# Expert stage of a hybrid encoder block: transposes placed inside the preceding product, splits on VectorE alone, two row blocks of each down matrix in full fp32

## The chip, the cores and the metric

The kernel runs on one core of a Trainium2 chip. Times are device microseconds (us) of one execution. Three runs of the kernel before gave 1526.49, 1527.76 and 1528.14 us; their median is 1527.76 us. In the text PE is TensorE (PEld its weight loads), DVE is VectorE, ACT is ScalarE, POOL is GpSimd, and SP is the engine whose queue issues most DMAs.

## The reference

One encoder layer on 1024 tokens of width 1024, all in float32. Three mixers (cross-attention to a memory, a convolution module, a bidirectional RWKV-7 recurrence) share one input projection and one output projection. Then comes the part that the change touches, a mixture of sixteen experts in which each expert picks its 128 tokens, and at last a norm:

```
h   = rms_norm(x)
aff = softmax(h @ w_router)                    # 1024 tokens x 16 experts
gates, idx = top_k(aff per expert, 128)
xe  = h[idx]                                   # 16 x 128 x 1024
hid = silu(xe @ w_gate) * (xe @ w_up)          # each w: 16 x 1024 x 1024
ye  = (hid @ w_down) * gates
x   = x + scatter_add(ye at idx)
y   = rms_norm(x)
```

## The kernel before, in words

The mixers, the output projection and the router's products come first; they fill the span up to about 860 us. Nothing there is touched. Then each expert's tokens are chosen (L1361 to L1407), which is a chain of short VectorE instructions, and the sixteen experts follow one by one.

**Products.** Every expert has three products of 128 rows with a 1024x1024 matrix: gate, up and down. A product takes eight steps k, one for each block of 128 rows of the matrix, and in each step two halves n of 512 columns. Both factors are split into a high part h and a rest l of the type float32r, and `mm3` (L331 to L333) adds three products: high x high, high x rest, rest x high. So one product has 8 x 2 x 3 = 48 matmuls and one expert 144. A matmul of two plain float32 factors is not split.

**Weights.** `fetch_w` (L1250) loads 256 rows of a matrix (1 MB) into one of twelve rooms `eraw`, in a fixed rotation, from SP's queue; the rooms hold one expert's twelve loads. The generator `parts` (from L1341) makes the two parts of each block of 128 rows: ScalarE copies the high part `ewh` (L1351, L1355), and the rest `ewl` is a subtraction. For gate and up it is always VectorE's (L1356, with the norm's gain). For down the subtractions alternate between VectorE and POOL (L1352). There are five buffers each of `ewh` and `ewl`, so the splits run up to five steps ahead of PE. The first five are made by L1360, ahead of the choice of tokens in the program.

**Rows.** `fetch(e)` makes a one-hot matrix `oneh` on VectorE (L1414), multiplies it with the token numbers and gates (L1418, eight small matmuls), copies the index and the gates on VectorE (L1419, L1420), and gathers the rows `xe` with an indirect DMA from POOL (L1422). `transposed` turns 128 rows into the stationary factor of a product: eight PE transposes into two PSUM banks (L1434), and for each bank ScalarE's high part (L1436, `xh` or `fh`) and VectorE's rest (L1437, `xl` or `fl`).

**Order.** For expert e the program has: the up product; the gating `hid` (L1545, two halves on VectorE, which read the up product's PSUM); the transposes of the next expert's rows; the fetch of the rows of expert e + 2; the gate product of expert e + 1 with its silu on ScalarE (L1458); the transposes of the gated product; the down product; ScalarE's scaling by the gates `ye` (L1471) and an indirect DMA from POOL that adds the rows to `x2_d` in DRAM (L1472). A planner orders the instructions of each engine ahead of time by the order of the program and by its own costs; on the chip each engine runs its own in that order.

**The end.** The gate product of the last expert is interrupted after four steps by the down product of the last but one. `last_loads` loads all rows of `x2_d` once that expert's rows have been added (L1493), and the last matrix. While the last products run, the rows are squared (L1506, L1508), scaled on VectorE (L1513) and stored (L1517). After the last down product, `last_norm` does the same for the last expert's 128 rows (L1523 to L1529).

Of the kernel before, what the change touches and what calls it, by code (L numbers as in the profile page):

```python
# [12 lines left out]
F32 = mybir.dt.float32  # L13
# [74 lines left out]
GD = 2  # L88
NPRE = 2
NBOR = 0  # L90
# [8 lines left out]
PF1 = 9  # L99


@with_exitstack
def hybrid_block_kernel(ctx: ExitStack, tc: tile.TileContext, x, xT, memT, memn, w_in, w_mk, w_mv, pcols,
# [14 lines left out]
    # ---------------------------------------------------------------- constants  # L118
# [16 lines left out]
    # mask of the within-chunk matrices, [rows s (twice), {strict, inclusive}, t]  # L135
    mask = const.tile([P, 2, C], F32, name="mask")
    V.memset(mask, 1.0)
    for hf in range(2):
        r = slice(hf * 64, hf * 64 + 64)
        for q in range(2):  # L140
            # keeps t - s - 1 + q >= 0
            G.affine_select(out=mask[r, q, :], in_=mask[r, q, :], pattern=[[1, C]], compare_op=ALU.is_ge, fill=0.0,
                            base=q - 1, channel_multiplier=-1)
# [8 lines left out]
    # masks that put the inverses of the diagonal blocks in place: [row, parity, block column]  # L152
# [19 lines left out]
    # identity columns as the lanes of the inversion hold them: [lane (quadrant, parity, chunk), sigma, t]  # L172
# [5 lines left out]
    # derived per-channel columns  # L178
# [27 lines left out]
    def rsqrt(dst, src, scale, eps):  # L206
        """dst = (src * scale + eps) ** -0.5: a first guess from the exponent, then Newton's steps."""
# [18 lines left out]
    def run(mains, fills):  # L226
        """mains: names in order; fills: name -> (pieces, number, first, last, needs); pieces of fills are spread over
        the mains' steps. needs: (own piece, name, count)"""
# [24 lines left out]
    # tiles that live through the whole first part  # L253
# [4 lines left out]
    # ---------------------------------------------------------------- projections  # L258
# [16 lines left out]
    # the even taps, the odd ones, and their sums  # L275
# [59 lines left out]
    # memory: keys and values  # L335
# [3 lines left out]
    def memory():  # L339
# [15 lines left out]
        # a bank's first product alone starts it: where nothing was written yet, the others' first ones do not add  # L355
# [76 lines left out]
    def ev_shift(nm, j):  # L432
        st = {}

        def f(ps, n, sl):
# [6 lines left out]
            if n == 1:  # L442
# [3 lines left out]
                if nm in shifted:  # L446
                    # rows 64-127 belong to the backward scan: reversed time
# [8 lines left out]
                if nm == "gd":  # L456
                    # twice the sigmoid
# [15 lines left out]
    # the first two projections follow the loads  # L473
# [30 lines left out]
    # ---------------------------------------------------------------- convolution  # L504
# [3 lines left out]
    def taps(eng, i, j):  # L508
        """one of the three half-rate filters of a tile of channels: even taps on even tokens, odd on odd, and
        their sums on neighbours' sums"""  # L510
# [17 lines left out]
    def conv():  # L528
        for i in range(3):
# [8 lines left out]
            # even tokens, then odd ones  # L538
# [50 lines left out]
    def keep(i, n):  # L589
        """a part of the mixers' output, split in two, to DRAM"""  # L590
# [8 lines left out]
    # ---------------------------------------------------------------- attention  # L599
# [47 lines left out]
    # ---------------------------------------------------------------- RWKV-7  # L647
    # The backward scan is the forward one on reversed time: its tiles hold time reversed, so one step serves both.
# [7 lines left out]
    def early():  # L656
        """what the first chunks need, in the room of the convolution and the attention"""
# [9 lines left out]
        # zeros stand where one head's rows meet the other head's columns  # L667
# [10 lines left out]
        # restart marks of the running sums  # L678
# [6 lines left out]
    def late():  # L685
        """the rest, in the room of the projections"""
# [6 lines left out]
        # of these two, the last half pair needs the second only  # L693
# [9 lines left out]
    def swap():  # L703
        """room for the output projection, for the last half pair"""
# [29 lines left out]
    def chunks(ap, d):  # L734
        """[P, 512] as [P, chunk, t], in the time of direction d"""
        ap = ap if d == 0 else ap[:, ::-1]
        return ap.rearrange("p (a b) -> p a b", b=C)
# [3 lines left out]
    def spread(rs):  # L741
        """[P tokens, 4 tiles, head] to [channels, 512 tokens] in PSUM"""
# [8 lines left out]
    def columns(src, two, ps=None):  # L751
        """512 tokens' products with two columns, tokens on partitions"""
# [24 lines left out]
    def prep(p, k, g):  # L777
# [7 lines left out]
        for d in range(2):  # L785
# [23 lines left out]
            # 1/P overwrites the running sums  # L809
# [4 lines left out]
            # -kk a / P  # L814
# [8 lines left out]
            # the even head's rows hold k before b, the odd one's b before k  # L823
# [16 lines left out]
    def bonus(p):  # L840
        # each token's r . k of both directions, weighed by r_k
# [5 lines left out]
    def within(g):  # L847
        """within-chunk matrices"""
# [13 lines left out]
    def prep2(p, k, g):  # L862
        BT = g["BT"] = Z["BT"][g["u"] % 2]
        SV = g["SV"] = Z["SV"][g["u"] % 2]
        for d in range(2):
            n = k if d == 0 else 1 - k
            # b and k with tokens on partitions
# [7 lines left out]
            # values with tokens on partitions: rows 0-63 the even head, rows 64-127 the odd one  # L875
# [13 lines left out]
    def invert(g):  # L889
        # inverses of the 32 x 32 diagonal blocks of I - A, one block and column parity per lane  # L890
# [9 lines left out]
        # lanes (quadrant, parity, chunk): [t, s]  # L900
        Lt = Z["ew"].tile([P, 32, 32], F32, name="Lt", bufs=1)
        V.transpose(Lt.rearrange("p a b -> p (a b)"), Ld[:, :, None, :].to_broadcast([P, 32, 2, NCH]))
        Dt = Z["ew"].tile([P, 16, 32], F32, name="Dt", bufs=1)      # [sigma, t]
# [12 lines left out]
        # back to rows s, columns t, both parities placed by the masks  # L916
# [9 lines left out]
        # the first block, not transposed  # L926
# [84 lines left out]
    def gated(p, n, pl, g):  # L1011
        """the gate with the norm's weight, and with what stands beside the norm"""
# [12 lines left out]
    def normed(p, ns, gl, out):  # L1025
        """both halves' (or one's) group norm, what stands beside it, the gate, and the split for the last product"""
# [42 lines left out]
    def residual():  # L1069
        """x plus the part of the output projection that the attention and the convolution give"""  # L1070
# [85 lines left out]
    def routed(dst, src):  # L1156
        """the products of 128 rows with the router's weights"""
# [464 lines left out]
```

## Time and profile before

| | |
|---|---|
| median of three runs | 1527.76 us (1526.49 to 1528.14) |
| span of the profiled execution, first to last instruction | 1526.2 us |
| TensorE busy | 1341.4 us |
| VectorE busy | 1230.6 us |
| ScalarE busy | 841.9 us |
| POOL busy | 458.8 us |
| moved by DMA | 327.92 MB |

The profiled execution is one of its own; of its time the page has the span, and the median of the three runs lies 1.6 us above that. Matmuls are pipelined: a matmul's duration holds the run-out of its results, and where they follow each other the distance of their starts is what one costs. A row of the timeline merges equal instructions that follow each other (x8). What stands in brackets is the idle time of the engine just before, and what ended it. A row of the waits has who waited, for whom, us in total, how often, and the longest.

### The profile page before, as it was taken

The numbers are of one execution on the slowest core, as the hardware profiler recorded it, in microseconds if no ns is written. First come the engines' busy times: TensorE is split into PE (matmuls) and PEld (weight loads), VectorE is DVE, ScalarE is ACT, GpSimd is POOL, SyncE is SP. The second block draws the span as 40 slices with busy tenths as digits, with TensorE's granted clock in tenths as the row PEclk, the third lists the DMA queues.
The fourth block names the chain that finished last, engine by engine and source line by source line (L and its number), as shares of the span: only waits on it lengthen the run. The fifth ranks groups of instructions, "written<-read, shape, count | busy, mean of one in ns | idle before, by whom it ended". The sixth has DMA issues, their size and how long they took to land.

```text
span 1526.2 us, 24448 instructions
## 1 busy us (share of the span) xinstructions
PE 1341.4 (88%) x9254; PEld 1074.2 (70%) x9254; DVE 1230.6 (81%) x2071; ACT 841.9 (55%) x1209; POOL 458.8 (30%) x302
## 2 busy tenths in 40 slices
PE   6988999996889898788999279999999999999984
PEld 4776658675777777667778167777777777777763
DVE  8899975698686979697534879888888888888887
ACT  4222574434435353424312358888888888888872
POOL 2233313432121213121211004444444444444323
PEclk9998899997897988899899679999999999999996
DMA  8222113313443524333525769999999999999855
GB/s 287 73 63 65 57 63 130 126 56 117 115 139 96 155 93 137 105 111 116 206 115 227 297 223 329 367 361 361 365 367 361 368 370 355 364 365 368 323 174 225
DMA packets 146101, 327.92 MB, mean 215 GB/s; under 512 B 9792, under 2 KB 64960, under 8 KB 145984
## 3 DMA queue, kind: packets, MB, share of 16 engines
q1 hardware_dynamic: 139360, 303.14, 55.3%
q0 software_dynamic: 6192, 22.55, 5.2%
q8 instruction: 72, 1.18, 0.3%
q10 hardware_dynamic: 432, 0.68, 0.1%
q14 instruction: 45, 0.37, 0.1%
HBM read 288.58 MB, written 37.75 MB: 214 GB/s over the span
## 4 chain that ended last, share of the span: by engine, by line
PE 55%; DVE 23%; ACT 8%; DMA 6%; issue 5%; POOL 1%; SPq 0%; POOLq 0%; DVEq 0%; ACTq 0%
PE mm L331 14%; PE mm L333 14%; PE mm L332 13%; DVE cv L519 3%; DVE dtmp L912 3%; DVE Dt L913 2%; DMA fo<-oT_d 2%; ACT Ld L897 2%; DVE ewl L1356 1%; ACT hid L1458 1%; ACT ewh L1351 1%; PE mm L1167 1%; PE mm L747 1%; DMA eraw<-in_w_ed_dram 1%; PE psA L856 1%
## 5 line engine op out<-in xcount | busy, mean ns | idle before, releaser
L1356 DVE SCALAR_TENSOR_TENSOR ewl<-eraw,pc,ewh 128x1024 fp32r<-128x1024 f32 x256 | 336.3, 1362 | 20.4 <-ACT ewh L1355 18.8
L1355 ACT ACTIVATE ewh<-eraw,pc 128x1024 fp32r<-128x1024 f32 x256 | 290.4, 1152 | 72.2 <-PE mm L333 70.1
L1352 POOL TENSOR_TENSOR ewl<-eraw,ewh 128x1024 fp32r<-128x1024 f32 x64 | 183.6, 2874 | 131.9 <-ACT ewh L1351 115.8
L331 PE MATMUL mm<-ewh,xh 128*128 128x512 f32 x512 | 201.6, 394 | 12.6 <-ACT xh L1436 12.6
L332 PE MATMUL mm<-ewl,xh 128*128 128x512 f32 x512 | 199.8, 390 | 0.0
L333 PE MATMUL mm<-ewh,xl 128*128 128x512 f32 x512 | 198.1, 392 | 0.1
L1351 ACT ACTIVATE ewh<-eraw 128x1024 fp32r<-128x1024 f32 x128 | 136.0, 1064 | 44.9 <-PE mm L333 39.0
L1352 DVE TENSOR_TENSOR ewl<-eraw,ewh 128x1024 fp32r<-128x1024 f32 x64 | 122.5, 1915 | 35.6 <-ACT ewh L1351 34.2
L331 PE MATMUL mm<-hh,wh 128*128 128x512 f32 x304 | 127.2, 419 | 9.8 <-ACT hh L312 9.8
L333 PE MATMUL mm<-hh,wl 128*128 128x512 f32 x304 | 126.5, 416 | 0.8 <-POOL wl L327 0.8
L332 PE MATMUL mm<-hl,wh 128*128 128x512 f32 x304 | 126.5, 416 | 0.4 <-DVE hl L313 0.3
L331 PEld LDWEIGHTS mm<-ewh,xh 128*128 128x128 f32 x512 | 96.3, 188 | 36.2 <-ACT xh L1436 16.5
L331 PE MATMUL mm<-ewh,fh 128*128 128x512 f32 x256 | 102.7, 403 | 14.3 <-ACT fh L1436 8.5
L332 PEld LDWEIGHTS mm<-ewl,xh 128*128 128x128 f32 x512 | 96.4, 188 | 19.6
L333 PEld LDWEIGHTS mm<-ewh,xl 128*128 128x128 f32 x512 | 95.0, 188 | 19.5 <-DVE xl L1437 0.6
L332 PE MATMUL mm<-ewl,fh 128*128 128x512 f32 x256 | 102.1, 399 | 7.0 <-DVE ewl L1352 7.0
L333 PE MATMUL mm<-ewh,fl 128*128 128x512 f32 x256 | 99.1, 397 | 1.8 <-DVE fl L1437 1.8
L327 POOL TENSOR_TENSOR wl<-wraw,wh 128x512 fp32r<-128x512 f32 x38 | 59.1, 1559 | 126.7 <-ACT wh L326 109.0
L1422 POOL DMA_INDIRECT xe<-h_d,idx x16 | 29.4, 1836 | 217.0 <-DVE gates L1420 217.0
L967 POOL TENSOR_TENSOR sps<-S,pcs 128x128 f32<-128x128 f32 x48 | 22.8, 474 | 218.7 <-DVE S L993 115.4
L331 PEld LDWEIGHTS mm<-hh,wh 128*128 128x128 f32 x304 | 60.1, 198 | 26.2 <-ACT hh L312 10.4
L332 PEld LDWEIGHTS mm<-hl,wh 128*128 128x128 f32 x304 | 60.0, 197 | 18.5 <-DVE hl L313 3.0
(412 smaller groups left out, 3011.2 us busy)
## 6 DMA issues: line engine op xcount, KB each, us to landing
eraw<-in_w_eg_dram SPq DMA_DIRECT2D x64, 1024.0 KB, 8.6
eraw<-in_w_eu_dram SPq DMA_DIRECT2D x64, 1024.0 KB, 9.2
eraw<-in_w_ed_dram SPq DMA_DIRECT2D x64, 1024.0 KB, 5.7
fo<-oT_d SPq DMA_DIRECT2D x64, 320.0 KB, 3.9
wraw<-in_w_in_dram SPq DMA_DIRECT2D x38, 256.0 KB, 2.7
ld_k<-d_k SPq DMA_DIRECT2D x18, 256.0 KB, 3.3
ld_v<-d_v SPq DMA_DIRECT2D x18, 256.0 KB, 3.1
xk<-in_xT_dram SPq DMA_DIRECT2D x16, 256.0 KB, 4.7
```

The costliest lines, as they stand in the source:

```text
L327: G.tensor_sub(wl, raw, wh.bitcast(F32))
L331: T.matmul(ps, lhsT=lh, rhs=rh, start=first, stop=False)
L332: T.matmul(ps, lhsT=lh, rhs=rl, start=False, stop=False)
L333: T.matmul(ps, lhsT=ll, rhs=rh, start=False, stop=last)
L519: V.scalar_tensor_tensor(o[:, 0:ln], z, w, o[:, 0:ln], op0=ALU.mult, op1=ALU.add)
L897: A.copy(Ld[r_, :, c:c + 4].rearrange("p t c -> p c t"), g["AM", d, q][r_, :, h, 0, b * 32:b * 32 + 32])
L912: IE.tensor_tensor(tmp[:, sg, ts], lcol, drow, op=ALU.mult)
L913: IE.tensor_tensor(Dt[:, sg, ts], Dt[:, sg, ts], tmp[:, sg, ts], op=ALU.add)
L1351: A.activation(h, raw[a], AF.Copy)
L1352: eng.tensor_sub(l, raw[a], h.bitcast(F32))
L1355: A.activation(h, raw[a], AF.Copy, scale=gain)
L1356: V.scalar_tensor_tensor(l, raw[a], gain, h.bitcast(F32), op0=ALU.mult, op1=ALU.subtract)
```

## The change

It has three parts, and moves the first five splits.

1. The transposes of the next expert's rows are issued after step 3 of the up product (`KTX`), and those of the gated product after step 2 of the next expert's gate product (`KTH`), each within the product's matmuls. The fetch of the rows of expert e + 2 is issued after step 0 of that gate product (`KTF`). The last expert's gated product is transposed ahead of its down product, as before.
2. All subtractions of the splits are VectorE's.
3. The last two (`NWHOLE`) of the eight row blocks of each down matrix are not split. PE multiplies them as they were loaded, with an unsplit copy `fw` of the transposed rows that ScalarE makes, as plain float32 matmuls. They use no `ewh` or `ewl` buffer, and their room `eraw` is read by PE.
4. The first five splits are issued within `fetch(0)`, and on VectorE behind its L1420 (the gates of the first expert), rather than ahead of the choice of tokens.

Comments were taken out as well. The core of the diff:

```diff
-GD = 2
+NWHOLE = 2
+KTX, KTF, KTH = 3, 0, 2
...
             for a in range(2):
+                if src is w_ed and k2 * 2 + a >= KT - NWHOLE:
+                    yield raw[a], None
+                    continue
                 h, l = halves.pop(0) if halves else [ex.tile([P, FF], F32R, name=n, bufs=NWB) for n in ("ewh", "ewl")]
-                turn[0] += 1
-                eng = G if turn[0] % GD == 0 else V
                 if src is w_ed:
                     A.activation(h, raw[a], AF.Copy)
-                    eng.tensor_sub(l, raw[a], h.bitcast(F32))
+                    V.tensor_sub(l, raw[a], h.bitcast(F32))
...
-    split = [next(parts) for _ in range(NWB)]
+    split = []
...
         if e == 0:
             tc.keep_in_program_order(g)
+
+            with tc.issue_after(gs.ins):
+                split.extend(next(parts) for _ in range(NWB))
...
-    def transposed(src, nm):
-        h = ex.tile([P, KT, P], F32R, name=nm + "h", bufs=2 if nm == "x" else 1)
-        l = ex.tile([P, KT, P], F32R, name=nm + "l", bufs=2 if nm == "x" else 1)
+    def transposed(src, nm, whole=0):
+        h = ex.tile([P, KT - whole, P], F32R, name=nm + "h", bufs=2 if nm == "x" else 1)
+        l = ex.tile([P, KT - whole, P], F32R, name=nm + "l", bufs=2 if nm == "x" else 1)
+        w = ex.tile([P, whole, P], F32, name=nm + "w", bufs=1) if whole else None
...
-            s_ = slice(a * 4, (a + 1) * 4)
-            A.activation(h[:, s_, :], ps, AF.Copy)
-            V.tensor_tensor(l[:, s_, :], ps, h[:, s_, :].bitcast(F32), op=ALU.subtract)
-        return h, l
+            n = min(4, max(0, KT - whole - a * 4))
+            s_ = slice(a * 4, a * 4 + n)
+            if n:
+                A.activation(h[:, s_, :], ps[:, 0:n], AF.Copy)
+                V.tensor_tensor(l[:, s_, :], ps[:, 0:n], h[:, s_, :].bitcast(F32), op=ALU.subtract)
+            if n < 4:
+                i = a * 4 + n - (KT - whole)
+                A.copy(w[:, i:i + 4 - n], ps[:, n:])
+        return h, l, w
...
-                mm3(acc[n], xh[:, k, :], xl[:, k, :], h[:, sl], l[:, sl], k == 0, k == KT - 1)
+                if l is None:
+                    T.matmul(acc[n], lhsT=xw[:, k - KT + NWHOLE], rhs=h[:, sl], start=k == 0, stop=k == KT - 1)
+                else:
+                    mm3(acc[n], xh[:, k, :], xl[:, k, :], h[:, sl], l[:, sl], k == 0, k == KT - 1)
...
-        product(up, *cur, then)
+        else:
+            then = {KTX: [lambda: turn_x(e + 1)]}
+        product(up, *xs.pop(e), then)
...
-            cur = transposed(rows.pop(0), "x")
+            then = {KTF: [lambda: bring(e + 2)] if e + 2 < NE else [], KTH: [lambda: turn_h(e, done)]}
             if e + 2 < NE:
-                rows.append(fetch(e + 2))
-                hid = gate(e + 1, cur)
-                add_back(e, done)
+                hid = gate(e + 1, xs[e + 1], then)
+                add_back(e, hs.pop(e))
```

`turn_x(e)` is `transposed` of the rows of expert e, `turn_h` that of the gated product with `whole=NWHOLE`, and `bring` is `fetch`.

## Rows read from the trace of the kernel before

**Rows 1.** The page, part 1: busy us (share of the span) and instructions of each engine.

```profile
PE 1341.4 (88%) x9254; PEld 1074.2 (70%) x9254; DVE 1230.6 (81%) x2071; ACT 841.9 (55%) x1209; POOL 458.8 (30%) x302
```

**Rows 2.** Busy time by window, one expert's period (columns in the first line).

```profile
core 0: us, PE busy (x) PEld busy (x) DVE busy (x) ACT busy (x) POOL busy (x), PEclk, DMA share, GB/s
1066.98:1104.60 37.62, 36.19 (x169) 29.55 (x168) 33.27 (x30) 30.76 (x32) 15.59 (x6) 1.00 1.01 364
```

**Rows 3.** Timeline of PE, end of an up product: start us, us, instruction, [idle before].

```profile
1095.08 0.39 PE L331 MATMUL mm<-ewh,xh 128*128 128x512 f32 x1
...
1104.37 0.39 PE L333 MATMUL mm<-ewh,xl 128*128 128x512 f32 x1
1104.60 1.03 PE L1434 MATMUL mm<-ident,xe 128*128 128x128 f32 x8
1106.48 0.50 PE L331 MATMUL mm<-ewh,xh 128*128 128x512 f32 x1 [0.85 <-ACT xh L1436]
1106.82 0.40 PE L332 MATMUL mm<-ewl,xh 128*128 128x512 f32 x1
...
1107.72 1.05 PE L1418 MATMUL mm<-tokaff,oneh 128*128 128x6 f32 x8
1108.63 0.70 PE L333 MATMUL mm<-ewh,xl 128*128 128x512 f32 x2
```

**Rows 4.** Timeline of PE, from a gate product to a down product.

```profile
1118.74 1.03 PE L1434 MATMUL mm<-ident,hid 128*128 128x128 f32 x8
1120.33 0.50 PE L331 MATMUL mm<-ewh,fh 128*128 128x512 f32 x1 [0.55 <-ACT fh L1436]
```

**Rows 5.** Waits from 960 to 1500 us: us in total, times, longest.

```profile
ACT ewh L1355 <- PE mm L333: 62.2, 150, 2.9
...
DVE ewl L1356 <- ACT ewh L1355: 14.5, 28, 0.7
...
PE mm L331 <- ACT xh L1436: 10.9, 13, 0.9
```

**Rows 6.** Timeline of PE, down product of the last but one expert.

```profile
1455.62 0.72 PE L333 MATMUL mm<-ewh,fl 128*128 128x512 f32 x2 [1.75 <-DVE fl L1437]
```

**Rows 7.** Timeline of VectorE, from the end of an up product on.

```profile
1104.47 1.40 DVE L1545 SCALAR_TENSOR_TENSOR hid<-mm,gates,hid 128x512 f32<-128x512 f32 x2
...
1112.90 2.48 DVE L1356 SCALAR_TENSOR_TENSOR ewl<-eraw,pc,ewh 128x1024 fp32r<-128x1024 f32 x2
1115.29 1.22 DVE L1352 TENSOR_TENSOR ewl<-eraw,ewh 128x1024 fp32r<-128x1024 f32 x1
1117.31 2.54 DVE L1352 TENSOR_TENSOR ewl<-eraw,ewh 128x1024 fp32r<-128x1024 f32 x1 [0.80 <-ACT ewh L1351]
```

**Rows 8.** Unsplit fp32 products: the group of L558, and two of its instructions.

```profile
L558 PE MATMUL mm<-oT,o 128*128 128x512 f32 x12 | 5.8, 605 | 0.0
...
228.09 0.59 PE L558 MATMUL mm<-oT,o 128*128 128x512 f32 x1
...
228.52 0.59 PE L558 MATMUL mm<-oT,o 128*128 128x512 f32 x1
```

**Rows 9.** Weights' loads from 1000 to 1440 us; a window with the queues undisturbed.

```profile
DMA to landing us min/median/max: 4.8/7.5/11.0
...
1106.00:1114.00 8.00, 7.48 (x36) 6.01 (x37) 7.12 (x9) 4.89 (x6) 1.84 (x1) 1.00 1.03 417
```

**Rows 10.** Timeline of VectorE, POOL and PE ahead of the first product.

```profile
879.86 6.06 DVE L1356 SCALAR_TENSOR_TENSOR ewl<-eraw,pc,ewh 128x1024 fp32r<-128x1024 f32 x5
...
886.28 1.87 POOL L1422 DMA_INDIRECT xe<-h_d,idx  x1 [31.56 <-DVE gates L1420]
...
891.63 1.94 PE L1434 MATMUL mm<-ident,xe 128*128 128x128 f32 x8 [2.45 <-DMA xe<-h_d,idx]
```

**Rows 11.** The last matrix: the chain's DMA; VectorE's groups from 1491.05 to 1513.75.

```profile
1476.76 15.42 DMA eraw<-in_w_ed_dram
...
L1513 DVE SCALAR_TENSOR_TENSOR eraw<-eraw,fr,gfi 128x1024 f32<-128x1024 f32 x8 | 14.2, 1805 | 0.0
L1352 DVE TENSOR_TENSOR ewl<-eraw,ewh 128x1024 fp32r<-128x1024 f32 x4 | 9.2, 2291 | 0.0
```

More of the change, by code (lines that the diff above doesn't have):

```diff
@@ L1332, in hybrid_block_kernel @@
     ex = pool("ex", bufs=2, side="right")
-    turn = [0]
     halves = [[ex.tile([P, FF], F32R, name=n, bufs=NWB) for n in ("ewh", "ewl")] for _ in range(NWB)]
@@ L1419, in fetch @@
         V.tensor_copy(idx[:, e:e + 1], ps[:, 0:1])
-        V.tensor_reduce(gates[:, :, e], ps[:, 1:5].rearrange("p (a b) -> p a b", b=2), axis=AX.X, op=ALU.add)
+        gs = V.tensor_reduce(gates[:, :, e], ps[:, 1:5].rearrange("p (a b) -> p a b", b=2), axis=AX.X, op=ALU.add)
         xe = ex.tile([P, D], F32, name="xe")
@@ L1434, in transposed, with product @@
                 T.transpose(ps[:, j, :], src[:, (a * 4 + j) * P:(a * 4 + j + 1) * P], ident)
-            s_ = slice(a * 4, (a + 1) * 4)
-            A.activation(h[:, s_, :], ps, AF.Copy)
-            V.tensor_tensor(l[:, s_, :], ps, h[:, s_, :].bitcast(F32), op=ALU.subtract)
-        return h, l
-    def product(acc, xh, xl, then=None, ks=range(KT)):
+            n = min(4, max(0, KT - whole - a * 4))
[7 more added lines that the diff above has]
+        return h, l, w
+    def product(acc, xh, xl, xw, then=None, ks=range(KT)):
         for k in ks:
@@ L1448, in product, with gate @@
                     f()
-    def gate(e, xs, between=None):
+    def gate(e, xs, then=None, between=None):
         ga = [mm("cx") for _ in range(2)]
         if between:
-            product(ga, *xs, ks=range(2 * BRK))
+            product(ga, *xs, then, ks=range(2 * BRK))
             between()
-        product(ga, *xs, ks=range(2 * BRK if between else 0, KT))
+        product(ga, *xs, then, ks=range(2 * BRK if between else 0, KT))
         hid = ex.tile([P, FF], F32, name="hid", bufs=2)
@@ L1459, in gate, with down @@
         return hid
-    def down(e, done, then=None):
-        hs = transposed(done, "f")
+    def down(e, hs, then=None):
         dn = [mm() for _ in range(2)]
@@ L1465, in down, with add_back @@
         return dn
-    def add_back(e, done):
-        dn = down(e, done)
+    def add_back(e, hs):
+        dn = down(e, hs)
         ye = ex.tile([P, D], F32, name="ye", bufs=1)
@@ L1530, in last_norm, with turn_x, turn_h, bring @@
                              in_offset=None)
-    rows = [fetch(0), fetch(1)]
-    cur = transposed(rows.pop(0), "x")
-    hid = gate(0, cur)
+    rows = {0: fetch(0), 1: fetch(1)}
+    xs, hs = {0: transposed(rows[0], "x")}, {}
+    def turn_x(e):
+        xs[e] = transposed(rows.pop(e), "x")
+    def turn_h(e, done):
+        hs[e] = transposed(done, "f", NWHOLE)
+    def bring(e):
+        rows[e] = fetch(e)
+    hid = gate(0, xs[0])
     for e in range(NE):
         up = [mm("y0"), mm("y1")]
-        then = None
         if e == NE - 1:
@@ L1547, in hybrid_block_kernel @@
         if e + 1 < NE:
-            cur = transposed(rows.pop(0), "x")
+            then = {KTF: [lambda: bring(e + 2)] if e + 2 < NE else [], KTH: [lambda: turn_h(e, done)]}
             if e + 2 < NE:
-                rows.append(fetch(e + 2))
-                hid = gate(e + 1, cur)
-                add_back(e, done)
+                hid = gate(e + 1, xs[e + 1], then)
+                add_back(e, hs.pop(e))
             else:
-                hid = gate(e + 1, cur, lambda: (add_back(e, done), last_loads()))
+                hid = gate(e + 1, xs[e + 1], then, lambda: (add_back(e, hs.pop(e)), last_loads()))
         else:
@@ L1557, in hybrid_block_kernel @@
             then[OGK].insert(0, own_gather)
-            dn = down(e, done, then)
+            dn = down(e, transposed(done, "f", NWHOLE), then)
     with tc.manual_schedule():
```

## The prediction

> **What bounds the kernel now.** I read the page first: over the span TensorE is busy 88%, VectorE 81%, ScalarE 55% [rows 1]. The change touches the sixteen experts and the two ends of that stage, so the question is what sets the pace there. The window from one expert's row transposes to the next is 37.62 us long, at a granted clock of 1.00, with PE busy 36.19, VectorE 33.27, ACT 30.76 and a DMA share of 1.01 [rows 2]. Three resources look full; the timeline of PE and the waits tell them apart.
>
> PE issues its split products without a hole: 41 steps from 1095.08 to 1104.37, 0.2266 us each [rows 3]. 144 of them are 32.63 of the 37.62. The other 5.0 lie at the boundaries. The eight transposes of the next rows start at 1104.60 and the first matmul behind them at 1106.48, 1.88 later, of which 0.85 is a wait for ScalarE's copy xh; that matmul takes 0.34 instead of 0.23, another 0.11. The one-hot products of the next list take from 1107.72 to 1108.63, 0.91, and start some 0.2 late. The transposes of the gated product take from 1118.74 to 1120.33, 1.59, with a wait of 0.55 for fh [rows 4], and 0.1 again. These make 4.8, with the products 37.4. So PE, in its own order, sets the pace. Among the waits PE's for xh comes 13 times in the window, once per expert; VectorE's splits wait for ACT, and ACT's for PE to free a buffer, 150 times [rows 5]: both follow PE.
>
> **The change, part by part.** *Transposes inside the product before.* PE still runs 16 per expert, but does not stand behind them. Eight cost at most the group's 1.03 with its run-out, and the eight one-hot products, with matmuls right behind them, 0.91 [rows 3]; I take 0.9. For x that saves 1.88+0.11-0.9 = 1.09 us, for 15 experts 16.4. For the hidden rows 1.59+0.11-0.9 = 0.80, for 14 experts 11.2. The fifteenth has a worse boundary: 1.75 more of waiting for fl [rows 6], which stood on VectorE behind a split; 0.8+1.75 = 2.6 saved. What hides the new waits: the transposes of x come with four of eight steps left, 5.4 us of matmuls, against copies and subtractions of some 2.4; those of the hidden rows come after three steps (3 x 6 x 0.2266 = 4.1) of the next gate product, while VectorE's gating, 1.40, starts as the up product ends [rows 7], so they are ready with 2.7 in hand. If that cover goes, PE waits in the midst of the product, with every later matmul behind it. The list's fetch moves behind the first gate step; its one-hot work and its gather stay, and I count its 0.2 of lateness as staying.
>
> *Two of eight row blocks of each down matrix unsplit.* Per block and half, three steps (0.68) go and one full fp32 product comes. The convolution's norm has such products (L558): two halves by three tiles are 6 in the program and 12 instructions in the trace, so each is two; back to back they step by 0.43, from 228.09 to 228.52 [rows 8]. 0.86-0.68 = 0.18, four times per expert 0.72: for the fifteen experts of the stage 10.8 lost. Bounds: 0.23 per instruction, the split step (0.9 per expert won), and the 0.6 that one lasts alone (2.1 lost). The step of 0.43 is measured back to back, as they will stand, so I take it.
>
> *Splits on VectorE alone.* POOL's four subtractions per expert go; VectorE has six instead of four. One takes 1.22 alone and 2.54 where POOL's overlapped it [rows 7], so the down splits take some 7.3 us per expert where four took about as much: nothing. ScalarE loses two copies and gains a short one. VectorE then has 16 splits of 1.24 (19.8), 7.3, gating 1.4, xl and fl 2.3, the one-hot 1.2 and small change: 32.3 in a period of 36.4. It is tightest over gate and up: 19.8+1.4+2.3+1.5 = 25.0 against PE's 16 x 1.36 + 2 x 0.9 + 0.9 = 24.5. The lead of five buffers, won back in each down product (7.3 against 8.2+3.4), covers the 0.5. So PE is late next, as before.
>
> *Weights.* Twelve rooms hold one expert's twelve loads, and a load is issued when its room comes free, a period ahead of its use. Landing takes 4.8 to 11.0 us [rows 9], so some 22 us are in hand. The last room of each down matrix is now freed by PE's read, not by a split, some 3 us later, and the loads behind it in SP's queue wait with it; that lessens the 22. The queues moved 417 GB/s over 8 us [rows 9] against the period's mean of 364 [rows 2]: its bytes need at least 37.62 x 364/417 = 32.8 us.
>
> The Trainium skill, SBUF — State Buffer, section "A bandwidth-pool intuition that's wrong (but worth ruling out)", puts the path from HBM to a core at about 358 GB/s and calls HBM almost always the bottleneck; by that 364 would be the ceiling and the period could not shrink. The 417 GB/s do not agree with it as a ceiling; what it would do here is the second rival.
>
> *Start.* VectorE does five splits (879.86, 6.06 us) ahead of the first list's index; the first gather starts at 886.28 and the first transposes at 891.63, after 2.45 of waiting for it [rows 10]. Put behind the index, the splits give back up to 4.0 us. But the second list's one-hot then stands behind them, and PE may run its products ahead of the transposes, which leaves 0.4. I take the middle, 2.2.
>
> *End.* The last matrix lands after a chain of DMAs (1476.76 plus 15.42) that PE does not set. From 1491 to 1513.8 VectorE never stops: 8 scalings, 14.2 us, and 4 splits, 9.2, beside POOL's [rows 11]. Without POOL, 8 at 1.24 and 6 at 1.22 are 17.2: 6 less. Against it, eight fp32 instructions after the last landing take 3.4, or 6.9 at the half clock. I take 5; bounds 0 and 6.
>
> **Sum.** 16.4+11.2+2.6-10.8 = 19.4 in the experts, 2.2 at the start, 5 at the end: 26.6. 1526.2-26.6 = 1499.6 of span. The median of the runs stands 1.6 above the profiled span: 1501.
>
> **Rivals.** (1) VectorE becomes the bound over gate and up: if its splits cost 1.32 there (POOL's address work for gather and scatter falls beside them), it is short by 0.5+1.3 = 1.8 per expert, more than the 1.2 won. 15 x 1.2 = 18 of the 26.6 go: 1519. For it: 33.27 of 37.62 busy. Against it: its splits wait for ACT today.
>
> (2) The loads hold their 37.6 us per expert whatever PE does. PE can run ahead by the 22 in hand, which its 21.6 of gain use up; then the end's loads queue behind late weights. Between 1506 (only the end's gain lost) and 1527 (all of it); 1514. For it, the share of 1.01; against it, the 417 GB/s.
>
> (3) Slower: the transposes in the product's midst stand too early in PE's order. They need the gating, and that stands on VectorE behind whatever splits the planner puts ahead of it, 1.24 each; the 2.7 in hand cover two. From the third PE waits; with four ahead 2.3 per expert, 1.1 more than is won, 14 x 1.1 less 7 at the ends: 1536; with six ahead 1570. Against it: the gating starts at once today [rows 7].
>
> (4) The planner, which orders by its own costs, leaves the transposes at the boundaries: the waits stay, fp32 costs 10.8, the ends give 7: 1531.
>
> (5) More than forecast: the one-hot's 0.2 goes in every expert, the start gives 4, the end 6: 1495, and to 1491 where the transposes hide further.
>
> **How the numbers follow.** The forecast, 1495 to 1510, has 0.60; (1) 0.13, (2) 0.08, (3) 0.05, (4) 0.05, (5) 0.09. The range of 1492 to 1518 leaves out (3) and (4) and the far ends of (1), (2) and (5). About 0.2%, 3 us, is what a measurement can tell from no change: of (4) a fifth and of (2) a tenth fall within it. Faster 0.88, same 0.02, slower 0.10.
>
> **What would show it.** After the change: 36.4 us between one expert's x transposes and the next (37.4 or more: wrong); no entry of PE waiting for xh or fh; fp32 instructions in steps of 0.43; down splits on VectorE at 1.22, none on POOL; later landings, but no wait of ACT or PE for a weight; the first gather up to 4 us sooner behind the first one-hot; VectorE through some 6 us sooner after the last matrix lands. The forecast is wrong if PE waits for ewl in the gate and up products, or stands before a transpose in their midst.

## The result, and the profile after

The changed kernel takes 1507.07 us (median; 1499.55 to 1507.65), the one before 1527.12 in the same runs: a ratio of 0.985, 95% interval 0.980 to 0.990. Forecast was 1501. The profiled execution's span is 1505.9 us, 20.3 less than before.

What lies ahead of the experts is the same code in both kernels, but its length varies from run to run (see the last section). So I compare from the first one-hot on VectorE (878.72 us before, 878.38 after) to the last instruction. In all tables here an expert ends where ScalarE's copy of its down product ends.

| stretch, us | before | after | gained | forecast |
|---|---|---|---|---|
| first one-hot to the first gate product | 14.7 | 14.2 | 0.5 | 2.2 |
| to the end of the 11th expert | 427.1 | 410.8 | 16.3 | 12.9 |
| the next four experts | 146.4 | 144.3 | 2.0 | 6.5 |
| from there to the end | 59.3 | 58.2 | 1.1 | 5 |
| sum | 647.5 | 627.6 | 19.9 | 26.6 |

(The forecast's 1.17 per expert, with 1.8 more for the fifteenth, is split as the rows are.) Page row and the window of one steady period, as in [rows 1, 2]:

```profile
PE 1346.2 (89%) x9190; PEld 1064.3 (71%) x9190; DVE 1191.3 (79%) x2103; ACT 806.2 (54%) x1193; POOL 264.2 (18%) x238
```

```profile
1086.00:1122.11 36.11, 36.11 (x165) 28.85 (x164) 31.50 (x31) 29.02 (x31) 3.43 (x2) 1.00 1.00 379
```

The period fell from 37.62 to 36.11, and PE is busy in all of it: the 1.4 us of holes are gone. From 1158 to 1303 us the waits hold no row of PE at all, where [rows 5] had PE waiting for xh once per expert. PE's timeline, at the transposes of x and at the unsplit blocks:

```profile
1090.57 1.03 PE L1443 MATMUL mm<-ident,xe 128*128 128x128 f32 x8
1091.36 0.48 PE L334 MATMUL mm<-ewh,xh 128*128 128x512 f32 x1
1091.67 0.40 PE L335 MATMUL mm<-ewl,xh 128*128 128x512 f32 x1
...
1117.78 3.59 PE L1460 MATMUL mm<-eraw,fw 128*128 128x512 f32 x8
1120.81 0.79 PE L334 MATMUL mm<-ewh,xh 128*128 128x512 f32 x1
1121.45 0.40 PE L335 MATMUL mm<-ewl,xh 128*128 128x512 f32 x1
```

The eight transposes hold the next matmul back by 0.79, where [rows 3] had 1.88, and no bracket stands behind them. The step after it is 0.31 instead of 0.23, so they cost 0.87 in all. From the first unsplit instruction to the second split one behind them are 3.67 us; less one split step of 0.23, eight instructions took 3.44, or 0.43 each.

At the start, VectorE, POOL and PE, as in [rows 10]:

```profile
881.77 6.06 DVE L1360 SCALAR_TENSOR_TENSOR ewl<-eraw,pc,ewh 128x1024 fp32r<-128x1024 f32 x5
887.75 1.22 DVE L1418 TENSOR_TENSOR oneh<-slots,posT 128x1024 fp32r<-128x1024 f32 x1
...
882.07 1.93 POOL L1426 DMA_INDIRECT xe<-h_d,idx  x1 [27.70 <-DVE gates L1424]
...
889.12 1.84 PE L1422 MATMUL mm<-tokaff,oneh 128*128 128x6 f32 x8 [7.53 <-DVE oneh L1418]
890.82 1.97 PE L1443 MATMUL mm<-ident,xe 128*128 128x128 f32 x8
```

The first gather is issued 3.7 us behind the first one-hot instead of 7.6, but PE's queue has the second list's one-hot products ahead of the transposes, and their one-hot stands behind the five splits.

At the end, SP's queue and PE:

```profile
1454.55 2.06 SPq L1509 DMA_DIRECT2D eraw<-x_d  x4
1456.70 0.46 SPq L1253 DMA_DIRECT2D eraw<-in_w_eu_dram  x1
...
1472.34 1.22 PE L334 MATMUL mm<-ewh,xh 128*128 128x512 f32 x2 [9.69 <-ACT ewh L1359]
```

The last block of the last up matrix is now issued behind the four loads of the x2 rows, which wait for the last scatter. Before, it was issued 20.1 us ahead of them (1453.91 against 1474.04). The program text is the same in both kernels (`NLR = 5`) and has this block behind the rows; the planner moved it ahead of them in the kernel before, and does not here. PE stands still 9.7 us in the up product for it.

In the last four experts, PE, ScalarE and VectorE; the first two rows of ScalarE are of a steady period. Below them are ScalarE's waits, the first line from 1122.1 to 1158.2 (steady), the others from 1342.1 to 1380.3:

```profile
1324.75 0.30 PE L1443 MATMUL mm<-ident,xe 128*128 128x128 f32 x1 [1.91 <-DMA xe<-h_d,idx]
...
1154.09 1.15 ACT L1359 ACTIVATE ewh<-eraw,pc 128x1024 fp32r<-128x1024 f32 x1 [0.20 <-PE mm L336]
1156.66 0.69 ACT L1487 ACTIVATE ye<-mm,gates 128x512 f32<-128x512 f32 x1 [1.43 <-PE mm L1460]
...
1371.29 1.14 ACT L1359 ACTIVATE ewh<-eraw,pc 128x1024 fp32r<-128x1024 f32 x1
1378.04 0.69 ACT L1487 ACTIVATE ye<-mm,gates 128x512 f32<-128x512 f32 x1 [5.60 <-PE mm L1460]
...
1379.80 1.28 DVE L1360 SCALAR_TENSOR_TENSOR ewl<-eraw,pc,ewh 128x1024 fp32r<-128x1024 f32 x1 [5.39 <-ACT ewh L1359]
```

```profile
ACT ewh L1359 <- PE mm L336: 4.3, 14, 1.1
...
ACT ye L1487 <- PE mm L1460: 5.6, 1, 5.6
...
ACT fh L1447 <- PE mm L1443: 2.9, 1, 2.9
...
ACT hid L1475 <- PE mm L336: 1.3, 1, 1.3
```

Two things differ from the steady experts. Single transposes of x stand right behind their gather, and PE waits 1.91 us in one. And ScalarE takes the copy of the down product (ye) after one or two splits of the next product instead of five, stands 5.6 us in it, and VectorE then waits as long for its next ewh. The copies fh and hid stand ahead of splits there too. In a steady period ScalarE waits at its splits, for PE to free a buffer; in this one it never does, so its splits no longer fill the buffers ahead of PE.

Four regular experts, less the half gate product that the last one lacks (24 steps), would take 139.0 us; these took 144.3. PE's waits in them sum to 3.9 of the 5.3: 1.9 for the gather, 1.0 for ewh and 1.0 for ewl.

### The profile page after: what moved, and what is told of

Same layout as the page of the kernel before. It is cut to its first block, busy times and chain, and to the rows that moved or that the text cites. A ratio compares the mean times of both kernels' runs of the same rounds, so it can differ in the third digit from the quotient of the medians.

```text
span 1505.9 us, 24196 instructions
## 1 busy us (share of the span) xinstructions
PE 1346.2 (89%) x9190; PEld 1064.3 (71%) x9190; DVE 1191.3 (79%) x2103; ACT 806.2 (54%) x1193; POOL 264.2 (18%) x238
## 4 chain that ended last, share of the span: by engine, by line
PE 59%; DVE 22%; DMA 7%; ACT 5%; issue 4%; POOL 1%; SPq 0%; POOLq 0%; DVEq 0%; ACTq 0%
PE mm L336 13%; PE mm L335 13%; PE mm L334 13%; DVE cv L522 3%; PE mm L1460 3%; DVE dtmp L915 2%; DVE Dt L916 2%; PE mm L1443 2%; ACT Ld L900 2%; DMA fo<-oT_d 2%; DMA eraw<-in_w_ed_dram 1%; PE psA L859 1%; PE mm L1170 1%; DVE BK L831 1%; PE psS L993 1%
## 5 line engine op out<-in xcount | busy, mean ns | idle before, releaser
L1360 DVE SCALAR_TENSOR_TENSOR ewl<-eraw,pc,ewh 128x1024 fp32r<-128x1024 f32 x256 | 319.8, 1280 | 73.0 <-ACT ewh L1359 65.9
L335 PE MATMUL mm<-ewl,xh 128*128 128x512 f32 x512 | 203.0, 396 | 3.0 <-DVE ewl L1360 2.9
L1356 DVE TENSOR_TENSOR ewl<-eraw,ewh 128x1024 fp32r<-128x1024 f32 x96 | 113.1, 1219 | 7.0 <-ACT ewh L1355 5.5
L336 PEld LDWEIGHTS mm<-ewh,xl 128*128 128x128 f32 x512 | 96.8, 189 | 20.1 <-DVE xl L1448 0.2
L1355 ACT ACTIVATE ewh<-eraw 128x1024 fp32r<-128x1024 f32 x96 | 98.6, 1058 | 13.3 <-PE mm L336 9.3
L1488 POOL DMA_INDIRECT x_d<-ye,idx x15 | 25.8, 1721 | 345.7 <-ACT ye L1487 345.7
L336 PE MATMUL mm<-ewh,fl 128*128 128x512 f32 x192 | 74.7, 390 | 1.1 <-DVE fl L1448 1.1
L335 PE MATMUL mm<-ewl,fh 128*128 128x512 f32 x192 | 75.5, 393 | 0.1
L334 PE MATMUL mm<-ewh,fh 128*128 128x512 f32 x192 | 73.3, 390 | 0.0
L522 DVE SCALAR_TENSOR_TENSOR cv<-u,cw,cv 128x512 f32<-128x512 f32 (+1 forms) x87 | 72.2, 860 | 0.1
L336 PEld LDWEIGHTS mm<-hh,wl 128*128 128x128 f32 x304 | 59.6, 196 | 17.1 <-POOL wl L330 3.8
```

Source lines behind the costliest of these rows:

```text
L334: T.matmul(ps, lhsT=lh, rhs=rh, start=first, stop=False)
L335: T.matmul(ps, lhsT=lh, rhs=rl, start=False, stop=False)
L336: T.matmul(ps, lhsT=ll, rhs=rh, start=False, stop=last)
L522: V.scalar_tensor_tensor(o[:, 0:ln], z, w, o[:, 0:ln], op0=ALU.mult, op1=ALU.add)
L1355: A.activation(h, raw[a], AF.Copy)
L1356: V.tensor_sub(l, raw[a], h.bitcast(F32))
```

## The experiments

The theory at the start: the gain is the placement of the transposes, and the shortfall is order, in SP's queue at the end, in PE's in the last four experts, and on VectorE at the start. In the headings, "from the first one-hot" is the time from there to the last instruction (before 647.5, after 627.6). Where no ratio is given, the kernel was run once, and what is said of it is read from that one trace.

### Order of the loads at the end: from the first one-hot 624.1

```
-NLR = 5
+NLR = 6
```

> One number changed: all four blocks of the last up matrix are issued ahead of the four loads of the x2 rows (six blocks instead of five). Theory A (the order of SP's queue took the end's gain): the block that now lands behind the x2 rows no longer waits for the last scatter, the product of the last expert's up matrix loses its stop of 9.7 us, the last transfer of the down matrix lands some 2.5 to 5 us earlier, and the time is 1502 to 1504.5 us against 1507.1 for the changed kernel. Rival B (the same bytes pass the queue behind the scatter either way, so the stop only moves from the up product to the down product): 1506 to 1508.

Ratio to the kernel before 0.986 (0.983 to 0.990). SP and PE at the end:

```profile
1415.62 7.96 SPq L1253 DMA_DIRECT2D eraw<-in_w_eu_dram  x4
...
1454.07 5.05 SPq L1253 DMA_DIRECT2D eraw<-in_w_ed_dram  x4
...
1469.61 1.22 PE L334 MATMUL mm<-ewh,fh 128*128 128x512 f32 x2 [5.41 <-ACT ewh L1355]
1473.57 0.80 PE L335 MATMUL mm<-ewl,fh 128*128 128x512 f32 x1 [2.74 <-DVE ewl L1356]
```

All four blocks are issued long before the scatter, and the stop in the up product is gone. Of its 9.7 us, 5.4 and 2.7 come back in the down product, whose blocks still stand behind the rows. All of PE's waits behind the 15th expert fall from 12.9 to 9.1, and 3.4 us are won from the first one-hot on. Theory A holds for the size, B for most of the stop.

### Splits behind the second one-hot: 625.2

```
-            tc.keep_in_program_order(g)
-            with tc.issue_after(gs.ins):
-                split.extend(next(parts) for _ in range(NWB))
+            tc.keep_in_program_order(g)
+        if e == 1:
+            with tc.issue_after(oh_.ins):    # oh_: this list's one-hot
+                split.extend(next(parts) for _ in range(4))
```

> Four of the first five weight splits are issued behind the second expert's one-hot on VectorE instead of all five ahead of it. Theory A (the start gained only 0.8 us because TensorE takes the second list's one-hot products ahead of the first transposes, and their one-hot stood behind five splits of 1.2 us): the first transposes start at 886.5 to 887.5 us instead of 890.8, the first gate product 4 us earlier than 892.6, the time 1503 to 1504. Rival B (the gather of the first rows or the split of xl, which then stands behind the moved splits, sets the start): under 1.5 us earlier, 1505.5 to 1507.

Ratio 0.985 (0.981 to 0.989). Its first one-hot is at 884.17:

```profile
887.86 1.87 POOL L1426 DMA_INDIRECT xe<-h_d,idx  x1 [27.70 <-DVE gates L1424]
...
893.15 1.94 PE L1443 MATMUL mm<-ident,xe 128*128 128x128 f32 x8 [2.39 <-DMA xe<-h_d,idx]
```

Against that mark the transposes start at 8.98 instead of 12.44, and now they wait for the gather: 3.5 us won at the start, 2.3 of them left at the end. Theory A holds, to the bound that the gather sets. The times expected in absolute terms could not be read, since the stretch ahead varies by more; the median of the whole runs, 1505.6, lies where B had it.

### Transposes of x held, then PE's whole order held: 627.0 and 629.8

```
-                T.transpose(ps[:, j, :], src[...], ident)
+                t = T.transpose(ps[:, j, :], src[...], ident)
+                if nm == "x":                 # second kernel: always
+                    tc.keep_in_program_order(t)
```

> The transposes of x are held in the place where the program text has them, in all experts. Theory A (the last four experts lost 6 us to transposes that were put, one by one, right behind their gather, and to what they displaced): the periods of the last four experts fall from 38.8, 38.2 and 37.4 to 36.1 to 36.6 us, no wait of TensorE for a gather is left, the time is 1500 to 1502. Rival B (these experts are slow since the loads' order changes near the end, whatever the transposes do): the periods stay above 37.3, the time above 1505. Rival C (the experts gain, but the stop at the last up block grows by as much, since its load and the x2 rows come by the same queue): the marks of the last downs are 6 us earlier, the time 1504 to 1507.

> The changed kernel with all transposes and all one-hot products of the experts held in the place where the program text has them, so that TensorE's order is the same in every expert. Theory A (what the last four experts still lost, 4 us with the transposes of x alone held, comes from the order of the work there: one-hot products and h transposes put earlier, and the splits that they displace): the last four periods fall from 144.3 us in all to 139.5 to 141, as four regular ones less the half gate product that is moved behind; from the first one-hot to the end 624 to 626 us against 627.6, since part of it is lost again in the stop at the last up block. Rival B (late transfers, whatever the order): 143 or more.

The second holds the experts' one-hot products as well. First kernel: ratio 0.986 (0.981 to 0.990); PE's waits from 1295 to 1438 us:

```profile
PE mm L335 <- DVE ewl L1360: 1.4, 3, 0.5
PE mm L334 <- ACT ewh L1359: 1.0, 1, 1.0
```

The wait for the gather is gone, and the last four experts take 143.2 instead of 144.3: the first of them fell from 38.7 to 36.3, the next two stayed at 38.0 and 37.7. With the whole order held they take 146.4, with a period of 40.5 among them. In that one the granted clock fell to 0.50, the 1.2 GHz level, for some 3 us, right after PE had waited 0.94 for ewl, and its split products step by 0.43 instead of 0.23:

```profile
1345.00:1346.00 1.00, 1.00 (x3) 0.78 (x3) 1.00 (x2) 0.00 (x0) 0.00 (x0) 0.50 0.87 311
```

A like fall in vector_alone, below, costs 1.6, so about 144.8 of the 146.4 would be left; that is an estimate. Either way PE's order is not what they lost: theory A fell in both. ScalarE and VectorE of the second kernel:

```profile
1366.30 0.69 ACT L1490 ACTIVATE ye<-mm,gates 128x512 f32<-128x512 f32 x1 [5.58 <-PE mm L1463]
...
1368.06 1.28 DVE L1360 SCALAR_TENSOR_TENSOR ewl<-eraw,pc,ewh 128x1024 fp32r<-128x1024 f32 x1 [5.36 <-ACT ewh L1359]
```

The copies of ye still stand ahead of the splits. Over the kernels with the moved transposes and VectorE alone, ScalarE's idle time ahead of the two copies of ye is 1.6 us in a steady period (none without unsplit blocks). In the periods of 37 to 41 us it is 2.5 to 6.5, with one exception of 0.7 (no_whole, 39.0, where PE has two lists' one-hot products and transposes in one period). But short periods near the end (35.1 to 36.3) have 0.9 to 5.3 as well. With the copies xh, fh and hid added, it is 6.5 to 13.4 in the long periods and 0.9 to 9.9 in those short ones. ScalarE's queue as a whole is a candidate, not a shown cause: its order was not held in a run.

### The parts alone: VectorE for all splits 643.1, ends 651.6, transposes alone 670.6, no unsplit blocks 619.8

Before, with every split on VectorE:

```
-GD = 2
+GD = 10 ** 9
```

> The kernel before with all splits on VectorE and nothing else changed. Theory A (the splits have slack away from the boundaries, so the engine does not matter there; at the boundaries the split of xl loses 0 to 0.4 us): steady period 37.3 to 37.6 against 37.6. Rival B (four more splits of 1.22 us each on an engine that is busy 33.3 of 37.6 us bind it): 38 or longer. Rival C (the slowing by GpSimd was what the boundaries cost): 36.9 or shorter.

Steady period 37.65; the window of one, and VectorE's groups from 1486.6 to 1510 us:

```profile
1130.42:1168.07 37.65, 36.21 (x170) 29.55 (x169) 34.37 (x34) 30.76 (x34) 3.43 (x2) 1.00 1.00 362
```

```profile
L1513 DVE SCALAR_TENSOR_TENSOR eraw<-eraw,fr,gfi 128x1024 f32<-128x1024 f32 x8 | 10.1, 1282 | 0.0
L1352 DVE TENSOR_TENSOR ewl<-eraw,ewh 128x1024 fp32r<-128x1024 f32 x8 | 9.5, 1220 | 0.0
```

In a steady period it is worth nothing (37.65 against 37.62), although four more splits per expert moved to VectorE. Its busy time grew by 1.1 only, since a down split takes 1.22 and no longer 1.84 in the mean, and one of gate and up 1.28 and no longer 1.36. At the end it is worth what was forecast: the scalings take 10.1 instead of 14.2 [rows 11], and the stretch behind the 15th expert 54.5 instead of 59.3. The first line here is from the 15th expert, the second from the 12th:

```profile
1453.94 0.73 PE L333 MATMUL mm<-ewh,fl 128*128 128x512 f32 x2 [0.18 <-DVE fl L1437]
...
1334.00:1335.00 1.00, 1.00 (x4) 0.81 (x3) 0.63 (x2) 0.36 (x1) 0.89 (x1) 0.50 0.94 356
```

The 15th expert's wait for fl, 1.75 in [rows 6], is 0.18 here with the transposes where they were, and its period 31.95 instead of 33.55. So these 1.6 us belong to VectorE's splits, not to the placement. The sum of the last four hides them (146.5 against 146.4), since the 12th period is 39.27: PE waits in it as in every other, but the granted clock was 0.50 for some 3 us, and eight split products step by 0.43.

The changed kernel with the transposes at the products' ends:

```
-KTX, KTF, KTH = 3, 0, 2
+KTX, KTF, KTH = 7, 0, 7      # h: 3 for the last but one expert
```

> The changed kernel with the transposes put back to the ends of the products (x behind the up product, h behind the gate product); splits on VectorE alone and the unsplit blocks stay. Theory A (the placement alone brings 1.9 us per expert, as the waits 1.09 and 0.80 of before): the steady period goes from 36.1 to 38.0 us, which is more than the 37.6 of before by what the unsplit blocks cost. Rival B (what made the boundaries dear was VectorE, slowed by GpSimd's subtractions beside it, and these are gone): the period is 36.5 to 37.2. Rival C (the unsplit blocks cost nothing since they relieve VectorE): 37.3.

Steady period 38.37. PE's timeline:

```profile
1113.05 1.03 PE L1443 MATMUL mm<-ident,xe 128*128 128x128 f32 x8
1114.93 0.50 PE L334 MATMUL mm<-ewh,xh 128*128 128x512 f32 x1 [0.85 <-ACT xh L1447]
1116.73 0.95 PE L1422 MATMUL mm<-tokaff,oneh 128*128 128x6 f32 x8
1127.20 1.03 PE L1443 MATMUL mm<-ident,hid 128*128 128x128 f32 x8
1128.78 0.50 PE L334 MATMUL mm<-ewh,fh 128*128 128x512 f32 x1 [0.55 <-ACT fh L1447]
```

The waits of [rows 3, 4] are back to the hundredth, 0.85 and 0.55, so in a steady period they never came from GpSimd beside VectorE (rival B fell). The period is 0.72 over that of vector_alone, which is what the unsplit blocks cost, and 2.27 over that of the changed kernel, which is what the placement is worth. Here all of the last experts keep the period, so their disorder comes with the transposes inside the products. At the end all eight blocks of the last up and down matrices are issued ahead of the x2 rows, and the stretch behind the 15th expert takes 53.8, the shortest of all these kernels:

```profile
1472.44 8.71 SPq L1253 DMA_DIRECT2D eraw<-in_w_ed_dram  x4
1491.07 2.13 SPq L1509 DMA_DIRECT2D eraw<-x_d  x4
```

The transposes alone, every second split of the down matrices on GpSimd:

```
-NWHOLE = 2
+NWHOLE = 0
...
-                    V.tensor_sub(l, raw[a], h.bitcast(F32))
+                    (V if a == 0 else G).tensor_sub(l, raw[a], h.bitcast(F32))
```

> The moved transposes alone: no unsplit blocks, and every second split of the down matrices on GpSimd as before. Theory A (the placement is the gain, and GpSimd's slowing of VectorE beside it is hidden): steady period 35.4 to 35.8. Rival B (VectorE, whose splits take 1.84 us beside GpSimd's instead of 1.22, falls behind over gate and up): 36 to 37 with waits for ewl.

Steady period 38.35, 0.7 longer than before, and 1560.6 us against 1531.6 beside it. A window, PE and VectorE:

```profile
1150.60:1188.95 38.35, 36.28 (x170) 29.35 (x169) 37.66 (x30) 30.61 (x33) 16.35 (x6) 1.00 0.97 355
```

```profile
1178.50 0.50 PE L336 MATMUL mm<-ewl,fh 128*128 128x512 f32 x1 [1.43 <-DVE ewl L1357]
...
1175.03 10.10 DVE L1357 TENSOR_TENSOR ewl<-eraw,ewh 128x1024 fp32r<-128x1024 f32 x3
```

VectorE is busy 37.66 of 38.35. Three of its down splits last 10.1 us in a row, 3.4 each beside GpSimd's, and PE waits for ewl in the down product. My own theory fell here: the placement gains only with the splits on VectorE alone.

The changed kernel without unsplit blocks:

```
-NWHOLE = 2
+NWHOLE = 0
```

> The changed kernel without unsplit blocks: all eight row blocks of the down matrix are split, on VectorE. Theory A (TensorE sets the period, the unsplit blocks cost 0.72 us by instructions and 0.40 us at the switch back): the steady period goes from 36.1 to 35.0 to 35.4 us. Rival B (VectorE binds: 31.5 us busy and two splits of 1.22 more, 34 of 35 us, with its waits): 36.1 or longer, with waits of TensorE for ewl. Rival C (the loads bind: 12.6 MB at the 379 GB/s that the steady periods of the changed kernel show with all queues busy): 36 with waits of ScalarE for eraw.

```profile
1119.30:1154.70 35.40, 35.40 (x170) 29.60 (x169) 33.70 (x34) 30.64 (x34) 3.44 (x2) 1.00 1.03 387
```

Steady period 35.37, PE without a hole; neither VectorE (33.7 busy) nor the queues (387 GB/s) bind. The blocks cost 0.74. The 0.40 that I had put down to a switch back is none: it is the rest of the eighth instruction, as the row at 1120.81 above showed. Over the whole stage it is 7.7 us better than the changed kernel, though its last stretch is 1.6 longer; 1501.5 us against 1531.6 beside it, one run each.

### How early the transposes of h may stand: 627.3

```
-KTX, KTF, KTH = 3, 0, 2
+KTX, KTF, KTH = 3, 1, 0
```

> The transposes of h after the first step of the gate product instead of the third (six matmuls of 0.227 us ahead of them instead of eighteen), the one-hot products behind the second step. Theory A (the cover is what counts: the gating of hid, two instructions of 0.74 us on VectorE behind a split in progress, isn't done after 1.4 us): TensorE waits for hid 0.5 to 2 us in each expert, the period goes from 36.1 to 36.6 to 38. Rival B (VectorE takes the gating at once): 36.1 to 36.3.

VectorE and PE:

```profile
1133.88 1.40 DVE L1573 SCALAR_TENSOR_TENSOR hid<-mm,gates,hid 128x512 f32<-128x512 f32 x2
...
1135.37 1.03 PE L1443 MATMUL mm<-ident,hid 128*128 128x128 f32 x8
1136.16 0.48 PE L334 MATMUL mm<-ewh,xh 128*128 128x512 f32 x1
```

Period 36.09: VectorE gates at once, its 1.40 end 0.1 before the transposes start, and nothing waits. Rival B holds; six matmuls are cover enough.

### The parts put together: 621.0, 631.6 and 630.6

Three edits (loads, splits, transposes of x held) in the changed kernel:

> The three edits together. If each of the three theories holds and they add: 1507 - 6 - 4 - 3.5 = 1493.5, range 1491 to 1497. If the end is bounded by the transfers behind the last scatter and the start by the gather: 1499 to 1503.

1501.3 us, ratio 0.984 (0.980 to 0.987); 6.5 us less than the changed kernel from the first one-hot. The start keeps its 3.5, the end its 3.1; the last four experts gain nothing. The second case expected is the nearer one. Then the same with `NWHOLE = 0` and PE's whole order held, and with `NLR = 8` besides:

> No unsplit blocks, order kept in all experts, the last up block ahead of the x2 rows, four of the first splits behind the second one-hot. If the parts add: from the first one-hot to the end 619.8 (no unsplit blocks) - 2.4 (start) - 3.3 (order of the loads) - 2.5 (order of the last experts) = 611.6 us, between 609 and 615; the time 1491 us, between 1487 and 1498. Rival (a faster experts' part only waits longer at the end for the transfers behind the last scatter): 616 and more.

> As the one before, and also the first two blocks of the last down matrix ahead of the x2 rows. Theory A (the last down product waits for its blocks behind the rows): its end comes 3 to 5 us earlier, the end 2 to 4 us. Rival B (the rows, which arrive that much later, and the square sums and scalings behind them set the end): 0 to 1 us, or later.

Ratios 0.989 (0.985 to 0.993) and 0.989 (0.986 to 0.992): by the traces worse than the parts. The first eight periods are 35.1 to 35.7, but from the ninth to the last but one they are 38.7 to 40.5, though PE has the same order in all of them. (In that of 40.5 the granted clock fell to 0.50 again.) ScalarE, and VectorE at the end before; the last line is ScalarE's of no_whole:

```profile
1381.04 1.27 ACT L1490 ACTIVATE ye<-mm,gates 128x512 f32<-128x512 f32 x2 [3.36 <-PE mm L336]
...
1344.51 6.07 DVE L1360 SCALAR_TENSOR_TENSOR ewl<-eraw,pc,ewh 128x1024 fp32r<-128x1024 f32 x5 [3.32 <-ACT ewh L1359]
...
1372.08 1.27 ACT L1487 ACTIVATE ye<-mm,gates 128x512 f32<-128x512 f32 x2 [4.09 <-PE mm L336]
```

Again ye stands ahead of the splits, behind one of the next product. But no_whole has the same there, with the longer wait, in a period of 35.9. Nor are late loads the cause, rival B of order_kept: no split waits for one in the long periods here, in those of order_kept, or in the last four experts of the changed kernel. What no_whole does not have is the held order. Its last four take 138.4 and these 148.1, while the loads and the moved splits alone changed them by 0 and 0.9. So holding PE's order is what most likely cost these 10 us. With the unsplit blocks it cost little (order_kept); why it costs so much without them is not shown.

Two blocks ahead of the rows bring 1.0 us, of which 0.4 is won at the start: the size that rival B gave.

The best by the trace is no_whole (619.8, one run); all_three has the best ratio of those timed (0.984), but its interval overlaps the changed kernel's. A version with no unsplit blocks, PE's order left free, and the loads and splits moved is what the experiments point to, and one with ScalarE's order held would test the open cause; neither was run.

## Why the prediction was right, and where not

The range held the time, and the mechanism forecast as the likeliest is the one that ran: PE sets the pace, its waits at the boundaries go, and it pays for the unsplit blocks. The sum was 6.7 us too large, by errors of both signs: the first eleven experts gained 3.4 more than forecast, the start, the last four and the end 10.1 less. That these partly cancel is luck. Two of the prediction's own signs of being wrong are there in the last four experts, where PE waits 1.0 us for ewl and stands 1.9 ahead of a transpose; from the second expert to the eleventh neither occurs.

- **Transposes**: forecast 1.09 and 0.80, together 1.89 per expert; measured 2.27 (turns_at_ends against the changed kernel). The difference is the lateness of the one-hot, 0.2, which I left standing and which rival (5) let go, and small steps beside it. But I priced this step by itself, and it has a condition: with half of the down splits on GpSimd it loses 0.7 (turns_alone).
- **Unsplit blocks**: forecast 0.72 from two instructions of 0.43 each; measured 0.74 (no_whole) and 0.72 (turns_at_ends against vector_alone). Right.
- **Splits on VectorE alone**: forecast at nothing in the experts and the whole gain at the end; vector_alone shows 0.03 us lost per steady period and 4.8 won at the end. But the 1.75 of the fifteenth boundary, counted with the transposes, belongs here: without GpSimd's splits 0.18 of it is left. What failed is that the end of the changed kernel did not keep it: the step counted only what VectorE saves, not that the planner, with other times, leaves the last up block behind the x2 rows in SP's queue. x2_behind_up gives 3.2 of it back in that stretch.
- **The 15 experts alike**: this failed. Eleven gained 16.3 us where 12.9 were forecast, the last four 2.0 where 6.5 were. The order in which the planner puts their work changed, in PE's queue and in ScalarE's, and it does so only with the transposes inside the products (turns_at_ends). PE's alone is not the cause (order_kept), late loads are not, and ScalarE's copies ahead of the next splits are a candidate; the cause stays open.
- **Start**: of 2.2 (between 0.4 and 4) the lower bound came, 0.5, for the reason given with it: PE ran the second list's products first. splits_late moves that and gains 3.5 there.
- **Rivals**: (1) VectorE is no bound even with eight down splits (no_whole), its splits at 1.28 over gate and up; the 1.24 in the prediction was one row's, the mean before was 1.36. (2) The loads are none: the queues moved 379 and 387 GB/s in the steady windows, against 364 before. The Trainium skill, SBUF — State Buffer, section "A bandwidth-pool intuition that's wrong (but worth ruling out)", gives the path from HBM to a core about 358 GB/s; these runs do not agree with that as a ceiling. (3) The transposes do not wait for the gating, not even with six matmuls ahead (h_turns_early). (4) was half true, at the end only: the planner moved the transposes, but forward, behind their gathers.

## What to carry to other kernels

Price an edit together with the ones that it needs: moved transposes gained 2.3 us per expert with VectorE alone on the splits and lost 0.7 with GpSimd beside it. Of a change in several parts run each without the others: here the unsplit blocks cost what the arithmetic said and bought nothing in the steady period. Where a planner writes the order, compare the first and the last repetitions of the loop in every queue, in those of the DMA and of the copying engine too; a gain shown in the steady state is not yet one at the end. Look at the granted clock of a period that is too long before its order is blamed.

## What the runs showed of the hardware

VectorE's subtraction of two 128x1024 tiles took 1.22 us alone and 3.4 beside GpSimd's (10.1 for three), so handing GpSimd four of 24 splits cost VectorE more than it took over (37.66 busy in turns_alone, 33.70 in no_whole). Unsplit fp32 products of 512 columns step by 0.43 us per instruction, two to a product, also between split ones, and with no price for the change of kind. In four kernels PE's granted clock fell from 2.4 to 1.2 GHz for 3 to 4 us in the midst of the steady products (vector_alone at 1333 us, order_kept at 1344, best_no_whole and best_two_ahead at 1281), and split products then stepped by 0.43 instead of 0.23. Three of these periods have like neighbours, and are 1.6 to 1.7 longer. In three of the four PE had just waited 0.9 for ewl, but the same wait one period later passed without a fall. What set these off is open; in turns_alone it fell at 948 in a longer stop, of 3.6 for ewl, for 7 us. And the stretch ahead of the experts, the same instructions in all kernels here, took 867.9 us up to the first one-hot in order_kept (mean granted clock of the run 0.932) and 888.2 in turns_alone (0.914): differences of a few us were only to be read from a mark inside the run.
